# Attention with softmax rows copied from SBUF to SBUF, fp32r transposes of the copies, and rotary tables read back from memory tile by tile

## The chip, the core and the metric

The kernel runs on one core of a Trainium2 chip. The metric is the device time of one execution in microseconds; the median of three runs before the change is 1856.83 us (1856.04 to 1858.79). The core has TensorE (PE, with its weight loads as PEld), VectorE (DVE), ScalarE (ACT), GpSimd (POOL) and SyncE (SP), which here only issues transfers. Tiles live in SBUF, results of matmuls in PSUM, inputs and spilled tensors in the chip's memory.

## The reference

One layer of a diffusion backbone on 1024 latent tokens with 256 context tokens and model width 1024. A token-mixing part has a gated recurrence (4 heads) and grouped-query attention side by side; a channel-mixing part sends tokens to 16 experts. The attention is what the change touches:

```python
def qk_norm(aq, ak):
    return rms_norm(heads(aq, ATT_HEADS), q_norm_g), rms_norm(heads(ak, ATT_KV_HEADS), k_norm_g)
...
xqa = apply_axial_rope(xqa, cos, sin)
xka = apply_axial_rope(xka, cos, sin)
keys = jnp.concatenate([cka, xka], axis=1)
vals = jnp.concatenate([cva, heads(xav, ATT_KV_HEADS)], axis=1)
...
def one_block(qi):
    s = jnp.einsum("bqhgd,bkhd->bhgqk", qi, k, preferred_element_type=jnp.float32) * scale
    p = jax.nn.softmax(s, axis=-1)
    return jnp.einsum("bhgqk,bkhd->bqhgd", p.astype(v.dtype), v)
```

There are 8 query heads of width 64 in 2 groups, and 1280 keys.

## The kernel before

The precision is kept by splitting an fp32 number into a high part rounded to fp32r and the remainder (`split`, L92 and L93: a cast on ScalarE, a subtraction on VectorE), and by three matmuls per product (`mm3g`, L176 to L178).

The attention stage works through 16 tiles: 8 blocks of 128 queries times 2 groups of 4 heads (`seq`). The score row of a head has 1280 columns, in three segments of 512, 512 and 256 (`SEG`). For a tile, `softmax` does, for one head, six score matmuls (L786), three maxima on VectorE (L788), and three exponentials on ScalarE (L795), each into an SBUF tile `p` of its segment; every segment has a ring of 5, 6 or 7 such tiles. `turn` j (ten per tile) transposes 128 columns of all four heads on TensorE, fp32 against `ident` (L804), into one PSUM tile, which is split into `pT`. `values` j multiplies the two parts with the values (L814). `back` and `out_turn` turn the tile's output.

The tiles overlap. A tile's loop has 24 steps i: an even i below 20 emits `turn` i/2; the steps i = 1, 6, 11, 16 (`SI`) emit `softmax` of heads 0 to 3 of the **next** tile; odd i from 5 on emit `values`; each step also emits some matmuls of independent work (`fill.run`: projections and the branches). So turn 0 of a tile comes right after the loop of the tile before, and it reads segment 0 of all four heads. Below, (h, a) is the exponential of head h and segment a; turns 0 to 3 read a = 0, turns 4 to 7 a = 1, turns 8 and 9 a = 2.

TensorE's order is the order in which the code is written. The other engines' orders come from a scheduler that goes by priorities; `tc.high_priority(offset=HP)` puts an instruction ahead. SyncE's queue issues transfers in order, so that an entry that waits holds up those behind it. A transfer's completion is counted by one of eight semaphores (`DMAHW0` to `DMAHW7`) that are used in turn.

Queries: `q_vec` loads a block's queries (`aq`), normalises them and rotates them with the tables `cq` and `sq` (cosine and sine times the gains), which stay in SBUF as two tiles of 256 KB; `q_turn` transposes the result (fp32r, against `identr`). Block 0 and 1 are rotated on VectorE, the others on GpSimd.

Of the kernel before, what the change touches and what calls it, by code (L numbers as in the profile page):

```python
# [28 lines left out]
def view(t, off, dims):  # L29
    """The tile's partitions with free dimensions [stride, size] from element off on."""  # L30
    a = t if isinstance(t, bass.AP) else t[:]
    return bass.AP(tensor=a.tensor, offset=a.offset + off, ap=[list(a.ap[0])] + [list(d) for d in dims])
# [13 lines left out]
def _layer(tc, nc, top, A, out):  # L46
# [35 lines left out]
    def rsqrt(pool, ss, n, scale, name):  # L82
        """(ss * scale + eps) ** -0.5"""
# [6 lines left out]
    def split(hi, lo, src, eng=None):  # L90
        """hi: src rounded to the parts' width; lo: what is left (exact)."""
        nc.scalar.copy(hi, src)  # L92
        (eng or nc.vector).tensor_tensor(lo, src, hi.bitcast(F32), op=OP.subtract)  # L93
# [3 lines left out]
    class Fill:  # L97
        """Matmuls of independent work, emitted between the steps of a dependent chain: the time is the tensor engine's."""
# [27 lines left out]
        def flushed(self):  # L126
            """The PSUM bank is on its way out: no matmuls into it for some steps."""
            self.wait = self.pause
# [7 lines left out]
    class Stream:  # L136
        """The weight chunks of the first sub-layer in the order of their use; each is loaded one chunk ahead."""
# [18 lines left out]
    def wload(src, kt, ncols, rowlen, off, hl=None):  # L156
        """A chunk of a weight: kt row tiles of 128, ncols columns from off on; as hi and lo."""
# [14 lines left out]
    def mm3g(p, a, b, nk, first=True, last=True):  # L172
        """p += sum over k of a[k].T @ b[k]; a, b: pairs of functions of k giving the hi and lo parts."""
# [15 lines left out]
    # the tokens, halves of them apart: [half][hi, lo]  # L189
# [15 lines left out]
    def natural(hi, lo, emit, tiles):  # L205
        """Token rows on the partitions: emit(token tile, PSUM); ctx tiles are 0, 1, x tiles 2 to 9."""
# [10 lines left out]
    def transposed(hi, lo, m, emit, ctx, halves=(0, 1)):  # L217
        """Features on the partitions: emit(first token, number of tokens, PSUM)."""
# [23 lines left out]
    with ExitStack() as st:  # L242
# [11 lines left out]
        # token tile t is loaded, normalised and transposed beside these row tiles of w_mod (9: after them)  # L254
# [51 lines left out]
        # rows 0, 1: the products with the hi parts of silu(c), silu(c_ctx); rows 2, 3: with the lo parts  # L306
# [64 lines left out]
    def rope_swap(o, x, s, eng):  # L371
        """o = x with the halves of each axis exchanged, times s; [128, heads, 64] each."""
# [4 lines left out]
    def gain_rows(rows, n):  # L377
        """A head's gains on all partitions, and the same with the halves of each axis exchanged."""
# [8 lines left out]
    lbp = consts.tile([128, 2, 4], F32, name="lbp")  # L387
    lb1 = consts.tile([128, 2, 4], F32, name="lb1")
    with ExitStack() as st:
        pool = st.enter_context(mkpool("right", name="sa", bufs=2))  # L390
        pps = st.enter_context(mkpool(name="saps", bufs=1, space=PSUM))
        # lower bounds: a softmax over the two layers' logits, its first component
# [19 lines left out]
        # keys: norm, rotary embedding; values as they are  # L412
# [63 lines left out]
        # the other adaLN parameters, as one row  # L476
# [33 lines left out]
        # their sums over the partitions, piece j of 512 on row j  # L510
# [20 lines left out]
    with ExitStack() as st:  # L531
# [41 lines left out]
        for i in range(2):  # L573
            for c in range(4):
                # of the last chunk the first half of the tokens first: it makes room
# [53 lines left out]
        def states(h, K, Z, acc, tt):  # L629
# [17 lines left out]
            def advance(d, i0, cs, kt):  # L647
# [3 lines left out]
                for i, c in enumerate(cs):  # L651
# [4 lines left out]
                    else:  # L656
                        # the state before the next chunk
# [51 lines left out]
    sOA = spill.tile([4, 128, T], F32, name="sOA")  # L709
    sBA = spill.tile([8, 128, T], F32, name="sBA")  # L710
    BA, BR, direct = [], [], [None]
# [6 lines left out]
    with ExitStack() as st:  # L718
# [15 lines left out]
        cq = pool.tile([128, 8, 64], F32, name="cq")  # L734
        sq = pool.tile([128, 8, 64], F32, name="sq")
        for i, (n, a) in enumerate((("c_cos", cq), ("c_sin", sq))):
            nc.scalar.dma_start(a, A[n].rearrange("(t p) c -> p t c", p=128))
            (nc.gpsimd, nc.vector)[i].tensor_tensor(a, a, rows[:, i:i + 1].to_broadcast([128, 8, 64]), op=OP.mult)
        QT, SC = {}, {}
# [3 lines left out]
        def q_vec(t):  # L743
            eng = nc.vector if t in QV else nc.gpsimd
            x = pool.tile([128, 8, 64], F32, name="aq", tag="aq")
            nc.sync.dma_start(x, sAQ[t].rearrange("p (h d) -> p h d", h=8))
            a = pool.tile([128, 8, 64], F32, name="qa", tag="qa")
# [8 lines left out]
            eng.tensor_tensor(a, x, cq[:, t:t + 1].to_broadcast([128, 8, 64]), op=OP.mult)  # L756
            rope_swap(b, x, sq[:, t:t + 1].to_broadcast([128, 8, 64]), eng)
# [16 lines left out]
        SEG = ((0, 512, 5), (512, 512, 6), (1024, 256, 7))  # L774

        def softmax(t, g, h):
# [16 lines left out]
            for a, (c0, n, bufs) in enumerate(SEG):  # L793
                p = pool.tile([128, n], F32, name="p", tag="p%d" % a, bufs=bufs)
                nc.scalar.activation(p, ss[a], AF.Exp, bias=m[:, 7:8], scale=sc, accum_out=SU[t, g][:, a, h:h + 1])  # L795
                PT[t, g, h, a] = p
            hp.__exit__(None, None, None)

        HL, PV = {}, {}

        def turn(t, g, j):
            p = ps.tile([128, 4, 128], F32, name="ptp", tag="pt", bufs=NPT)
            for h in range(4):
                nc.tensor.transpose(p[:, h], PT[t, g, h, j // 4][:, (j % 4) * 128:(j % 4 + 1) * 128], ident)  # L804
# [45 lines left out]
        def branch_in():  # L850
            """The first half of the tokens makes room for the first branch's input."""
# [41 lines left out]
        for h in range(4):  # L893
            softmax(0, 0, h)
            fill.run(F1)
        for n, (t, g) in enumerate(seq):
# [3 lines left out]
            for i in range(20 + LAG - 1):  # L900
# [12 lines left out]
                if nxt and i in SI:  # L913
                    softmax(*nxt, SI.index(i))
# [27 lines left out]
    with ExitStack() as st:  # L942
# [4 lines left out]
        # the router on x1: its weights take the norm's gain and the scale; the shift gives a row  # L947
# [21 lines left out]
        # merged branches: [hi, lo][row tiles 0-3, 4-7][tokens 0-511, 512-1023]  # L969
# [525 lines left out]
```

## Time and profile before

| what | before |
|---|---|
| median of the runs | 1856.83 us |
| the profiled execution, its span | 1854.5 us |
| TensorE busy, share of the span | 1731.6 us, 93% |
| VectorE busy | 1331.0 us, 72% |
| ScalarE busy | 995.4 us, 54% |
| GpSimd busy | 273.7 us, 15% |
| DMA, mean over the span | 207 GB/s |

The profile is that of one execution on the chip; its span runs from the first to the last instruction, and the run's time is a little longer. A busy TensorE means that matmuls are in flight there; they overlap, so the distance from one's start to the next one's start is what a matmul costs. In the time of attention, about 600 to 1012 us, the DMA engines are nearly empty, while in the experts' part behind it they carry some 370 GB/s.

### The profile page before, as it was taken

What the parts mean: (1) busy time and instruction counts of PE and PEld (TensorE: products, weight loads), DVE (VectorE), ACT (ScalarE), POOL (GpSimd) and SP (SyncE); (2) the same over time, 40 slices, a digit from 0 to 9 for tenths busy, and PEclk for the clock granted to TensorE, in tenths of its full rate; (3) what the DMA queues carried; (4) which work ended last, traced back from release to release, by engine and by line L of the source; (5) the groups of instructions that cost most, each with busy time, mean ns of one, the idle gap of its engine ahead of it and who ended that gap; (6) DMA issues with size and microseconds to landing.
All of it is one profiled execution on the core that took longest, in us unless ns stands there. A gap on an engine that the chain in (4) does not pass through costs nothing. (4 is left out here: it accounts for less than half of the span.)

```text
span 1854.5 us, 26192 instructions
## 1 busy us (share of the span) xinstructions
PE 1731.6 (93%) x9820; PEld 1454.9 (78%) x9820; DVE 1331.0 (72%) x2000; ACT 995.4 (54%) x1632; POOL 273.7 (15%) x241
## 2 busy tenths in 40 slices
PE   5899999999999799999999999939999999999995
PEld 2798887899988678787787788828888888887774
DVE  6656323876766466777875664469999999998897
ACT  6422331322323367777876532227777777777665
POOL 3400001020000201111100332140011001001103
PEclk9899999999999999999999999959999999999998
DMA  8285445353332410101212776459999999999972
GB/s 326 93 309 208 171 140 198 106 174 103 103 117 81 130 43 29 46 29 58 89 51 87 261 262 238 159 187 358 378 379 371 379 379 374 376 379 379 370 261 101
DMA packets 206319, 383.87 MB, mean 207 GB/s; under 512 B 17488, under 2 KB 65568, under 8 KB 202864
## 3 DMA queue, kind: packets, MB, share of 16 engines
q1 hardware_dynamic: 194944, 360.92, 54.4%
q0 software_dynamic: 4832, 19.34, 3.8%
q10 hardware_dynamic: 6416, 1.94, 0.4%
q8 instruction: 77, 1.26, 0.3%
q14 instruction: 50, 0.41, 0.1%
HBM read 323.02 MB, written 59.13 MB: 206 GB/s over the span
## 5 line engine op out<-in xcount | busy, mean ns | idle before, releaser
L93 DVE TENSOR_TENSOR elo<-eraw,ehi 128x1024 fp32r<-128x1024 f32 x378 | 452.2, 1221 | 22.2 <-ACT ehi L92 14.4
L92 ACT CAST ehi<-eraw 128x1024 fp32r<-128x1024 f32 x384 | 383.6, 1047 | 86.6 <-PE pgu L178 48.5
L177 PE MATMUL pgu<-elo,xeT 128*128 128x512 f32 x512 | 203.7, 398 | 2.8 <-DVE elo L93 2.4
L176 PE MATMUL pgu<-ehi,xeT 128*128 128x512 f32 x512 | 204.9, 400 | 0.2 <-ACT xeT L92 0.2
L178 PE MATMUL pgu<-ehi,xeT 128*128 128x512 f32 x512 | 202.4, 395 | 0.0
L176 PE MATMUL pj<-hx,whi 128*128 128x512 f32 x448 | 185.4, 414 | 6.5 <-ACT stg L69 5.3
L178 PE MATMUL pj<-hx,wlo 128*128 128x512 f32 x448 | 175.8, 392 | 0.0
L177 PE MATMUL pj<-hx,whi 128*128 128x512 f32 x448 | 175.5, 392 | 0.0
L795 ACT ACTIVATE p<-s,m,qsc 128x512 f32<-128x512 f32 (+1 forms) x192 | 134.3, 713 | 17.7 <-DVE m L792 17.5
L788 DVE TENSOR_REDUCE m<-s 128x1 f32<-128x512 f32 (+1 forms) x192 | 104.3, 596 | 48.5 <-PE s L786 48.2
L176 PE MATMUL pj<-whi,hx 128*128 128x256 f32 x448 | 130.9, 292 | 3.6 <-DVE stg L541 1.9
L92 ACT CAST pT<-ptp 128x512 fp32r<-128x512 f32 x160 | 92.7, 595 | 71.9 <-PE ptp L804 71.8
L178 PE MATMUL pj<-whi,hx 128*128 128x256 f32 x448 | 128.1, 286 | 1.4 <-DVE hx L93 1.3
L93 DVE TENSOR_TENSOR pT<-ptp,pT 128x512 fp32r<-128x512 f32 x160 | 108.3, 685 | 29.2 <-ACT pT L92 28.5
L177 PE MATMUL pj<-wlo,hx 128*128 128x256 f32 x448 | 127.4, 284 | 0.0
L177 PEld LDWEIGHTS pgu<-elo,xeT 128*128 128x128 f32 x512 | 96.3, 188 | 29.0 <-DVE elo L93 8.0
L176 PEld LDWEIGHTS pgu<-ehi,xeT 128*128 128x128 f32 x512 | 96.9, 189 | 21.8 <-ACT xeT L92 0.5
L178 PEld LDWEIGHTS pgu<-ehi,xeT 128*128 128x128 f32 x512 | 96.2, 188 | 22.6 <-DVE xeT L93 0.4
L1385 POOL DMA_INDIRECT ACC<-ye,idx x15 | 34.7, 2316 | 474.9 <-DVE ye L1384 474.9
L176 PE MATMUL pye<-ehi,hdT 128*128 128x512 f32 x256 | 104.8, 409 | 0.0
L177 PE MATMUL pye<-elo,hdT 128*128 128x512 f32 x256 | 102.1, 399 | 1.2 <-DVE elo L93 1.2
L814 PE MATMUL pv<-pT,vs 128*128 128x512 f32 x320 | 102.2, 403 | 0.9 <-DVE pT L93 0.8
(365 smaller groups left out, 3919.7 us busy)
## 6 DMA issues: line engine op xcount, KB each, us to landing
eraw<-in_w_exp_gate SPq DMA_DIRECT2D x64, 1024.0 KB, 12.0
eraw<-in_w_exp_up SPq DMA_DIRECT2D x64, 1024.0 KB, 11.6
eraw<-in_w_exp_down SPq DMA_DIRECT2D x64, 1024.0 KB, 12.2
wm<-in_w_mod SPq DMA_DIRECT2D x24, 1024.0 KB, 6.9
raw<-in_w_in SPq DMA_DIRECT2D x21, 1024.0 KB, 6.1
sFK<-sg SPq DMA_DIRECT2D x32, 256.0 KB, 2.3
sGT<-stg SPq DMA_DIRECT2D x32, 256.0 KB, 2.1
sgm<-sGT SPq DMA_DIRECT2D x32, 256.0 KB, 3.8
```

Of the source, the lines that this page charges most:

```text
L92: nc.scalar.copy(hi, src)
L93: (eng or nc.vector).tensor_tensor(lo, src, hi.bitcast(F32), op=OP.subtract)
L176: nc.tensor.matmul(p, a[0](k), b[0](k), start=s, stop=False)
L177: nc.tensor.matmul(p, a[0](k), b[1](k), start=False, stop=False)
L178: nc.tensor.matmul(p, a[1](k), b[0](k), start=False, stop=e)
L788: nc.vector.tensor_reduce(m[:, a:a + 1], s, axis=AX.X, op=OP.max)
L795: nc.scalar.activation(p, ss[a], AF.Exp, bias=m[:, 7:8], scale=sc, accum_out=SU[t, g][:, a, h:h + 1])
L814: nc.tensor.matmul(PV[t, g].rearrange("p a b -> p (a b)"), VS[:, g, j], hl[i], start=(j == 0 and i == 0), stop=(j == 9 and i == 1))
L1385: nc.gpsimd.indirect_dma_start(out=ACC, out_offset=bass.IndirectOffsetOnAxis(ap=idx[:, :1], axis=0), in_=ye, in_offset=None, compute_op=OP ...
```

## The change

Four things are done.

1. After the exponential, each tile `p` is copied by a transfer from SBUF to SBUF, issued by SyncE with high priority, into a tile `pr` (`relay`). The rings of 5, 6 and 6 buffers are now those of the copies; each exponential has a single buffer per segment, which comes free when its copy has landed. Most copies follow their softmax; three are issued later in the loop (`LATE`): (2,1) at step 15, (2,2) and (3,2) at step 19.
2. `turn` transposes the copies as fp32r against `identr`, by reading the same bits under that type.
3. The rotary tables are multiplied by the gains in temporary tiles (which borrow buffers of `pT1`) and stored to memory (`sRT`).
4. `q_vec` loads the 64 KB slice of its block (`cs`) and rotates with it.

```diff
-        cq = pool.tile([128, 8, 64], F32, name="cq")
-        sq = pool.tile([128, 8, 64], F32, name="sq")
-        for i, (n, a) in enumerate((("c_cos", cq), ("c_sin", sq))):
+        for i, n in enumerate(("c_cos", "c_sin")):
+            a = pool.tile([128, 8, 64], F32, name="rt", tag="pT1", bufs=3)
             nc.scalar.dma_start(a, A[n].rearrange("(t p) c -> p t c", p=128))
             (nc.gpsimd, nc.vector)[i].tensor_tensor(a, a, rows[:, i:i + 1].to_broadcast([128, 8, 64]), op=OP.mult)
+            nc.sync.dma_start(sRT[:, :, i].rearrange("t p c -> p t c"), a)
...
             nc.sync.dma_start(x, sAQ[t].rearrange("p (h d) -> p h d", h=8))
+            cs = pool.tile([128, 2, 64], F32, name="cs", tag="cs", bufs=2)
+            nc.sync.dma_start(cs, sRT[t])
...
-            eng.tensor_tensor(a, x, cq[:, t:t + 1].to_broadcast([128, 8, 64]), op=OP.mult)
-            rope_swap(b, x, sq[:, t:t + 1].to_broadcast([128, 8, 64]), eng)
+            eng.tensor_tensor(a, x, cs[:, :1].to_broadcast([128, 8, 64]), op=OP.mult)
+            rope_swap(b, x, cs[:, 1:].to_broadcast([128, 8, 64]), eng)
...
-        SEG = ((0, 512, 5), (512, 512, 6), (1024, 256, 7))
+        SEG = ((0, 512, 5), (512, 512, 6), (1024, 256, 6))
+        NEW = {}
+
+        LATE = {(2, 1): 15, (2, 2): 19, (3, 2): 19}
...
-                p = pool.tile([128, n], F32, name="p", tag="p%d" % a, bufs=bufs)
+                p = pool.tile([128, n], F32, name="p", tag="p%d" % a)
...
-                PT[t, g, h, a] = p
+                NEW[h, a] = t, g, p
             hp.__exit__(None, None, None)
+
+        def relay(h, a):
+
+            t, g, p = NEW.pop((h, a))
+            n = SEG[a][1]
+            r = pool.tile([128, n], F32, name="pr", tag="pr%d" % a, bufs=SEG[a][2])
+            with tc.high_priority(offset=HP):
+                nc.sync.dma_start(r, p)
+            PT[t, g, h, a] = r
...
-                nc.tensor.transpose(p[:, h], PT[t, g, h, j // 4][:, (j % 4) * 128:(j % 4 + 1) * 128], ident)
+                nc.tensor.transpose(p[:, h].bitcast(F32R), PT[t, g, h, j // 4][:, (j % 4) * 128:(j % 4 + 1) * 128].bitcast(F32R), identr)
...
                 if nxt and i in SI:
-                    softmax(*nxt, SI.index(i))
+                    h = SI.index(i)
+                    softmax(*nxt, h)
+                    for a in range(3):
+                        if (h, a) not in LATE:
+                            relay(h, a)
+                if nxt:
+                    for k, at in LATE.items():
+                        if at == i:
+                            relay(*k)
```

TensorE at the border of the seventh tile, before: the last values of the tile that ends, then turn 0, which reads segment 0 of four heads (`p_7217` is head 3's), then the scores of the following tile's head 0. In brackets stands what a row waits for.

```order
L814 MATMUL pv_7078<-pT_7233,vs_5357 128x512 [waits Activation_49]
L814 MATMUL pv_7078<-pT_7234,vs_5357 128x512 [waits DVE_49]
L804 MATMUL ptp_7272<-ident_71,p_7032 128x128 [waits PE_49]
L804 MATMUL ptp_7272<-ident_71,p_7104 128x128
L804 MATMUL ptp_7272<-ident_71,p_7158 128x128
L804 MATMUL ptp_7272<-ident_71,p_7217 128x128 [waits Activation_49]
L786 MATMUL s_7283<-kT_5355,qT_6939 128x512 x2
L786 MATMUL s_7287<-kT_5355,qT_6939 128x512 [waits Activation_49]
```

The same place after the change (`pr_7394` is the copy of head 3's):

```order
L830 MATMUL pv_7239<-pT_7408,vs_5358 128x512 [waits Activation_49]
L830 MATMUL pv_7239<-pT_7409,vs_5358 128x512 [waits DVE_49]
L820 MATMUL ptp_7453<-identr_78,pr_7193 128x128 [waits DMAHW7_49,PE_49]
L820 MATMUL ptp_7453<-identr_78,pr_7271 128x128 [waits DMAHW2_49]
L820 MATMUL ptp_7453<-identr_78,pr_7331 128x128 [waits DMAHW6_49]
L820 MATMUL ptp_7453<-identr_78,pr_7394 128x128 [waits DMAHW1_49]
L793 MATMUL s_7464<-kT_5356,qT_7084 128x512 [waits Activation_49]
L793 MATMUL s_7464<-kT_5356,qT_7084 128x512
```

TensorE's order is the same; the wait of the fourth transpose is for a transfer and no longer for ScalarE, and the other three have one too.

SyncE's queue before, around that border: stores of staged tiles, a query load and a weight chunk.

```order
L847 DMA sOA_5348<-stg_6604 128x2x128 [waits DMAHW0_49,Activation_49]
L70 DMA sGT_2588<-stg_6652 128x512 [waits DMAHW1_49,Activation_49]
L746 DMA aq_7251<-sAQ_2589 128x512 [waits DMAHW5_49,DMAHW2_49,Pool_49]
L70 DMA sGT_2588<-stg_6854 128x512 [waits DMAHW3_49,Activation_49]
L164 DMA raw_7761<-in_w_branch_a 128x4x512 [waits DMAHW4_49,DVE_49]
L847 DMA sOA_5348<-stg_6871 128x2x128 [waits Activation_49]
```

And after, the copies of heads 1, 2 and 3 of the seventh tile, with what lies between and behind them:

```order
L812 DMA pr_7271<-p_7265 128x512 [waits DMAHW2_49,PE_49,Activation_49]
L812 DMA pr_7273<-p_7267 128x512 [waits DMAHW3_49,Activation_49]
L812 DMA pr_7275<-p_7269 128x256 [waits DMAHW4_49,Activation_49]
L863 DMA sOA_5348<-stg_7308 128x2x128 [waits DMAHW5_49,Activation_49]
L812 DMA pr_7331<-p_7325 128x512 [waits DMAHW6_49,PE_49,Activation_49]
L812 DMA pr_7358<-p_7327 128x512 [waits DMAHW7_49,PE_49,Activation_49]
L812 DMA pr_7412<-p_7329 128x256 [waits DMAHW0_49,PE_49,Activation_49]
L812 DMA pr_7394<-p_7388 128x512 [waits DMAHW1_49,Activation_49]
L812 DMA pr_7396<-p_7390 128x512 [waits DMAHW2_49,Activation_49]
L812 DMA pr_7414<-p_7392 128x256 [waits DMAHW3_49,PE_49,Activation_49]
L70 DMA sGT_2588<-stg_7489 128x512 [waits DMAHW4_49,Activation_49]
L748 DMA aq_8017<-sAQ_2589 128x512 [waits DMAHW5_49,Pool_49]
```

Twelve copies a tile stand among the same stores and loads; the two late ones of head 2 (`pr_7358`, `pr_7412`) wait for TensorE and stand ahead of head 3's first.

VectorE at the start of attention, before: the sine table times the gains, the rotation of block 0, the remainder of its split (`qs`), then block 1.

```order
L738 TENSOR_TENSOR sq_5386<-sq_5386,rows_5379 128x512 [waits DMAHW5_49,DMAHW3_49,DMAHW7_49,DMAHW1_49,DMAHW0_49]
L375 TENSOR_TENSOR qb_5404<-aq_5391,sq_5386 128x16x16 [waits DVE_49]
L375 TENSOR_TENSOR qb_5404<-aq_5391,sq_5386 128x16x16
L758 TENSOR_TENSOR qa_5393<-qa_5393,qb_5404 128x512 [waits DVE_49]
L93 TENSOR_TENSOR qs_5409<-qa_5393,qs_5409 128x8x64 [waits Activation_49]
L748 TENSOR_TENSOR qa_5680<-aq_5678 128x512 [waits DMAHW1_49,DVE_49]
```

And after:

```order
L739 TENSOR_TENSOR rt_5390<-rt_5390,rows_5380 128x512 [waits DMAHW5_49,DMAHW3_49,DMAHW7_49,DMAHW1_49,DMAHW0_49]
L760 TENSOR_TENSOR qa_5398<-aq_5394,cs_5396 128x512 [waits DMAHW4_49,DVE_49]
L375 TENSOR_TENSOR qb_5409<-aq_5394,cs_5396 128x16x16 x2
L762 TENSOR_TENSOR qa_5398<-qa_5398,qb_5409 128x512 [waits DVE_49]
L93 TENSOR_TENSOR wlo_5550<-raw_5548,whi_5549 128x2048 [waits PE_49,Activation_49]
L93 TENSOR_TENSOR qs_5414<-qa_5398,qs_5414 128x8x64 [waits Activation_49]
```

The rotation now waits for the slice `cs` (`DMAHW4`), which in turn is loaded after both stores of `sRT`, and the remainder of a weight chunk (`wlo`) has come to stand ahead of `qs`.

## Rows read from the trace of the kernel before

**Rows 1.** Attention by engine: window, us, busy, PEclk, DMA share, GB/s.

```profile
657.00:1012.00 355.00, 347.88 (x1942) 282.90 (x1941) 259.95 (x585) 261.62 (x620) 37.44 (x38) 1.00 0.16 52
```

**Rows 2.** Groups in 657 to 1012: busy us, mean ns, idle before.

```profile
L804 PE MATMUL ptp<-ident,p 128*128 128x128 f32 x640 | 96.2, 273 | 3.3 <-DVE pT L93 2.8
```

**Rows 3.** TensorE's waits in 657 to 1012: total us, times, longest.

```profile
PE ptp L804 <- DVE pT L93: 2.8, 3, 1.7
...
PE pv L814 <- ACT pT L92: 0.2, 1, 0.2
```

**Rows 4.** Timeline of TensorE at a border: start, us, instruction, count.

```profile
765.17 1.42 PE L786 MATMUL s<-kT,qT 128*128 128x512 f32 x6
...
767.58 0.60 PE L804 MATMUL ptp<-ident,p 128*128 128x128 f32 x4
767.94 0.47 PE L176 MATMUL pj<-hx,whi 128*128 128x512 f32 x1
768.25 0.39 PE L177 MATMUL pj<-hx,whi 128*128 128x512 f32 x1
...
770.80 0.60 PE L804 MATMUL ptp<-ident,p 128*128 128x128 f32 x4
```

**Rows 5.** Timeline of TensorE where keys are transposed as fp32r.

```profile
269.89 0.46 PE L458 MATMUL ptk<-identr,kd 128*128 128x128 f32 x4
270.18 0.46 PE L176 MATMUL pj<-hx,whi 128*128 128x512 f32 x1
270.48 0.40 PE L177 MATMUL pj<-hx,whi 128*128 128x512 f32 x1
```

**Rows 6.** Timeline of ScalarE at the border of rows 4: (3,0).

```profile
768.70 0.79 ACT L795 ACTIVATE p<-s,m,qsc 128x512 f32<-128x512 f32 x1
769.38 0.20 ACT L795 ACTIVATION_READ_ACCUMULATOR p<-s,m,qsc 128x1 f32 x1
```

**Rows 7.** Timeline of ScalarE: (3,0) at the loosest and the tightest border.

```profile
834.26 0.82 ACT L795 ACTIVATE p<-s,m,qsc 128x512 f32<-128x512 f32 x1
...
993.89 0.78 ACT L795 ACTIVATE p<-s,m,qsc 128x512 f32<-128x512 f32 x1
```

**Rows 8.** Timeline of TensorE: turn 0 at these two borders.

```profile
838.08 0.60 PE L804 MATMUL ptp<-ident,p 128*128 128x128 f32 x4
...
995.30 0.60 PE L804 MATMUL ptp<-ident,p 128*128 128x128 f32 x4
```

**Rows 9.** Transfers in 657 to 1012: count, KB each, median us to landing.

```profile
sGT<-stg SPq DMA_DIRECT2D x14, 256.0 KB, 2.0
...
sOA<-stg SPq DMA_DIRECT2D x10, 128.0 KB, 1.8
aq<-sAQ SPq DMA_DIRECT2D x5, 256.0 KB, 2.7
raw<-in_w_in SPq DMA_DIRECT2D x1, 1024.0 KB, 5.2
...
stg<-sOA SPq DMA_DIRECT2D x4, 64.0 KB, 2.0
...
hd<-sMod SPq DMA_DIRECT2D x1, 8.0 KB, 1.5
```

**Rows 10.** Timeline of VectorE at the start of attention.

```profile
623.11 0.69 DVE L738 TENSOR_TENSOR sq<-sq,rows 128x512 f32<-128x512 f32 x1
...
624.63 0.69 DVE L758 TENSOR_TENSOR qa<-qa,qb 128x512 f32<-128x512 f32 x1
626.01 0.69 DVE L93 TENSOR_TENSOR qs<-qa,qs 128x512 fp32r<-128x512 f32 x1 [0.69 <-ACT qs L92]
...
636.67 2.28 DVE L93 TENSOR_TENSOR wlo<-raw,whi 128x2048 fp32r<-128x2048 f32 x1
```

**Rows 11.** Timeline of TensorE there: queries turned, first scores, a later wait.

```profile
628.10 0.79 PE L769 MATMUL ptq<-identr,qs 128*128 128x128 f32 x8
633.62 2.50 PE L786 MATMUL s<-kT,qT 128*128 128x512 f32 x6 [4.73 <-DVE qT L770]
...
645.51 0.50 PE L176 MATMUL pj<-hx,whi 128*128 128x512 f32 x1 [1.28 <-ACT stg L69]
```

More of the change, by code (lines that the diff above doesn't have):

```diff
@@ L710, in _layer @@
     sBA = spill.tile([8, 128, T], F32, name="sBA")
+    sRT = spill.tile([8, 128, 2, 64], F32, name="sRT")
     BA, BR, direct = [], [], [None]
@@ L913, in _layer @@
                 if nxt and i in SI:
-                    softmax(*nxt, SI.index(i))
+                    h = SI.index(i)
+                    softmax(*nxt, h)
+                    for a in range(3):
+                        if (h, a) not in LATE:
+                            relay(h, a)
+                if nxt:
+                    for k, at in LATE.items():
+                        if at == i:
+                            relay(*k)
                 fill.run(FB if BR else FA)
```

## The prediction

> **What bounds the kernel now.** I read the views in this order: the busy times of the attention stage, its costliest groups on TensorE, TensorE's waits there, the timelines of TensorE and ScalarE around the border between two tiles, the landing times of transfers, and the start of the stage. In the 355 us from 657 to 1012, which hold fifteen borders between the sixteen tiles, TensorE is busy for 347.88 us at full granted clock, VectorE and ScalarE for about 260 each, and the DMA engines carry 52 GB/s at a share of 0.16 [rows 1]. Its waits there are short: five groups that sum to 6.6 us, of 2.8, 1.7, 1.1, 0.8 and 0.2 [rows 3]. So the stage costs what its matmuls cost. A saving on TensorE counts in full, and so does any new wait of TensorE. That makes the border the place to look at: TensorE's order is fixed by hand, and its order there is score matmuls of head 3 of the next tile, fillers and value matmuls, then turn 0 of that next tile, which reads the exponentials of all four heads.
>
> **The transposes.** The 640 transposes of softmax rows are fp32 [rows 2]. Four of them start at 767.58 and the next matmul at 767.94, and that one's successor at 768.25: 0.36 + 0.31 = 0.67 us [rows 4]. A group of four fp32r transposes in the same position, also followed by L176 and L177, starts at 269.89, 270.18 and 270.48: 0.29 + 0.30 = 0.59 us [rows 5]. That is 0.08 us less for a group of four, and 160 groups give **-12.8 us**. The times are rounded to a hundredth, so I keep -10.5 to -15. All of it lies on the path, apart from what the borders take back.
>
> **The copies.** Each of the 192 exponential tiles gets a transfer from SBUF to SBUF, and what follows reads the copy. For most of them there is time: from border to border a tile takes 22.5 us ((995.30 - 838.08) / 7 [rows 8]), so its 24 steps take 0.94 each, and turns 4 and 8, which are the first to read the second and third segments, come 8 and 16 steps after turn 0. Turn 0 is different. At a typical border the exponential (3,0) runs from 768.70 to 769.49 and its accumulator is read out by 769.58 [rows 6]; turn 0 starts at 770.80 [rows 4], which is 1.31 us after the exponential ends. The same difference read at all fifteen borders is, in order, 1.31, 1.88, 1.40, 2.00, 1.31, 1.33, 1.79, 2.99, 1.31, 1.32, 1.02, 1.05, 1.88, 1.36, 0.63 us. The longest is from 834.26 + 0.82 on ScalarE to 838.08, the shortest from 993.89 + 0.78 to 995.30 [rows 7, 8]. In the changed order only the last of turn 0's four transposes reads head 3, and each of the four waits for its own transfer.
>
> No transfer from SBUF to SBUF stands in this trace. The nearest rows: stores of 256 KB land 2.0 us after issue, stores of 128 KB 1.8, loads of 256 KB 2.7, a load of 8 KB 1.5 [rows 9]. The copy is 256 KB and its source is SBUF like that of the 256 KB store, so I take 2.0 and keep 1.5 and 2.7 as ends. From the end of the exponential the copy needs 0.1 (accumulator), 0.2 (two handovers, an estimate) and the landing L. Three transposes that go ahead give 0.2 back, and the one turn between these points that has become shorter takes 0.08. So TensorE waits L + 0.18 less the slack, where that is positive. Summed over the fifteen slacks: 10.9 us for L = 2.0, 4.8 for 1.5, 8.2 for 1.8, 20.7 for 2.7. **+10.9 us.** Behind the waiting transpose stand, on TensorE, the score matmuls of the following tile's head 0 and all else, since that order is fixed; ScalarE and VectorE wait for these in turn.
>
> The Trainium skill, page "DMA: Bandwidth & Descriptors", section "Anatomy of one DMA — SWDGE (gpsimd) path", gives 2.0 us plus bytes over 436e3 per microsecond, 2.6 us for 256 KB (an estimate from that page), though for transfers issued another way. The trace's 256 KB stores land in 2.0, so the measurement speaks against the second part of the sum; by the page the wait would be about 19 us.
>
> **What the borders pay back.** A TensorE that pauses at turn 0 lets VectorE and ScalarE catch up, and the 6.6 us of waits for them [rows 3] shrink. I take about half, **-3 us** (0 to -6.6).
>
> **SyncE's queue.** All copies are issued by SyncE in order, together with the stores of staged tiles, the query loads and the weight chunks, and each waits for the transfer eight before it. Late copies are placed where their buffers have come free: (2,1) after turn 7, (2,2) after turn 9, both ahead of (3,0), and both turns end before that exponential does, so I see no standing block. The DMA engines at a share of 0.16 [rows 1] have room for the copies: 128 of 256 KB and 64 of 128 KB are 41.9 MB, in 355 us 118 GB/s. But a weight chunk of 1 MB, landing in 5.2 us [rows 9], would hold up a copy at a border by up to 3.2 us if it falls there. Five such chunks in the stage, and a chance of about 5.2 of 22.5 us for each, with stores in front of a copy now and then: **+2 us** (0 to +6). More waits on one instruction and ScalarE's exponentials, which now wait until the copy from the single buffer has landed (for (3,2) about 2 to 3 us after turn 9, just long enough): **+0.5** (0 to +2.5).
>
> **The rotary tables.** Before, the sine table's product ends at 623.80, tile 0's queries are rotated by 625.32 and split by 626.70, and TensorE turns them at 628.10, when it gets to it [rows 10, 11]. Now the product is stored (256 KB, 2.0) and a 64 KB slice comes back (2.0) [rows 9]: about 628.4 with handovers. Three products, 0.7 to 0.8 each, end at 630.6. In the changed order the 2.28 us remainder of a weight chunk (`wlo`, at 636.67 before [rows 10]) stands ahead of the queries' remainder, which ends near 633.6. TensorE turns then instead of at 628.10, and the first scores start near 635.6 instead of 633.62: +2.0. Of the 1.28 us at 645.51, a wait for a ScalarE copy [rows 11] that the changed order puts earlier, some 0.5 goes. **+1.5 us** (-1 to +5). The slices of later tiles come beside a 256 KB query load that takes longer, so they cost nothing; without that cover each would cost under 2 us, seven times.
>
> **Sum.** -12.8 + 10.9 - 3.0 + 2.0 + 0.5 + 1.5 = -0.9 us. The profiled execution spans 1854.5 us and the median of the runs is 1856.8, so 2.3 us lie around the span and stay: **1855.9 us**.
>
> **The rivals.** What a measurement of this kernel can tell from no change is about 0.2%, 3.7 us.
> First, the forecast: the border gives back nearly what the transposes win. Chance 0.41 (about 0.35 within 0.2%, 0.03 on each side).
> Second, the copy lands sooner than a store, in 1.5 to 1.8 us; for it speaks that neither end is in memory, against it that the only row below 1.8 carries 8 KB. Then the border costs 4.8 to 8.2 and the time is 1849.8 to 1853.2, say 1851. Chance 0.32, nearly all faster.
> Third, slower: the copies land like the 256 KB loads, 2.7 us, at every border. One mechanism: the last transpose of turn 0 waits 1.57 us at a typical border. It decides from L of about 2.3, where the border's cost passes 15 us and the sum is above +3.5. The sum becomes -12.8 + 20.7 + 1 = +8.9 and the time 1865.7. For it: 192 copies more than triple what the DMA engines carry; against it: at 52 GB/s even stores of that size land in 2.0. Chance 0.18. The Trainium skill's formula from the page named above would land here, at 2.6 us.
> Fourth, SyncE's order: a copy (3,0) stands at every border behind a store that waits for ScalarE, a microsecond each, +15 in all: 1870.9. Chance 0.05.
> Fifth, the change does not do what it says: fp32r transposes on copied data step like fp32 ones, 0.67 us for four. The 12.8 is lost: 1868.7. The key transposes at 0.59 speak against it. Chance 0.04.
>
> **How the numbers follow.** Faster by over 0.2%: 0.29 + 0.03 = 0.32. Slower by over 0.2%: 0.15 + 0.05 + 0.04 + 0.03 = 0.27. The rest, 0.41, is within. The range of the likeliest case alone is 1852 to 1860; the range over the cases goes from the second's lower end, with a little more from the transposes, to just past the third: 1848 to 1867.
>
> **What would show it.** Copies near 2.0 us in the list of transfers. In the timeline of TensorE a gap of 0.5 to 1.2 us before the last transpose of turn 0, put down to the transfer `pr<-p`, at twelve or more borders, and waits for transfers near 11 us in all. Groups of four transposes at 0.59 with their follower. The first scores about 2 us later than before, measured from the sine product. Wrong would be: no such waits (the second), waits near 20 us (the third), gaps on SyncE behind stores (the fourth), fours that still take 0.67 (the fifth). A longer stage with no waits on TensorE at the borders would overturn the whole reading.

## The result

The changed kernel takes 1872.65 us (median of 4 runs, 1871.05 to 1876.09), the kernel before in the same comparison 1856.43; the ratio is 1.0085, with a 95% interval of 1.0070 to 1.0101. That is 16.2 us slower, 13.0 to 18.8 by the interval. The prediction was 1855.9 us, no change, with a range of 1848 to 1867; the result lies above the range, and where the sum had -0.9 us the kernel became slower.

The profiled execution spans 1872.3 us, 17.8 more than before. Since TensorE runs its matmuls in the same order in both kernels, the timelines can be laid on each other matmul by matmul. Up to the 25th matmul ahead of the first turn of queries, a point shortly ahead of attention, the changed kernel is 4.1 us behind, from there to the last softmax transpose it loses 13.4 (387.7 us before, 401.1 after), and behind that 0.3. The 4.1 us lie in code that the change leaves alone. They come mostly with stretches at the lower granted clock, one early in the program and one from 617 us on, and in the other kernels of this study, which have the same code there, the same point comes between 0.8 us earlier and 9.0 us later than in the kernel before. So all comparisons of traces below are made on the attention stretch, from that 25th matmul to the last transpose.

TensorE in attention by engine as in [rows 1] (window, us, busy of PE, PEld, DVE, ACT, POOL, clock, DMA share, GB/s), from the first turn of softmax rows to the last, before and after:

```profile
657.50:1009.10 351.60, 344.48 (x1925) 280.15 (x1924) 258.91 (x583) 260.94 (x617) 37.44 (x38) 1.00 0.16 52
661.80:1026.60 364.80, 340.71 (x1925) 269.48 (x1924) 260.73 (x584) 262.57 (x619) 37.52 (x38) 1.00 0.46 160
```

TensorE is busy for 3.8 us less and the stretch is 13.2 longer all the same: it stands idle for 24 us, where it was 7. The waits of TensorE there, which answer to [rows 3] (waiting tile and line, what ended the wait: total us, times, longest):

```profile
PE ptp L820 <- DMA pr<-p: 12.4, 15, 1.9
PE s L793 <- ACT p L802: 5.3, 7, 1.2
PE ptp L820 <- DVE pT L93: 3.1, 3, 1.9
PE pj L176 <- ACT stg L69: 1.1, 4, 0.4
PE pv L830 <- DVE pT L93: 0.8, 2, 0.6
PE ptp L820 <- DVE m L799: 0.7, 3, 0.2
PE pv L830 <- ACT pT L92: 0.3, 1, 0.3
```

The first row is new, the second has grown from 1.7, the rest is near what it was. A border looks like this in the timeline of TensorE (start, us, instruction, count, idle time before and its releaser):

```profile
683.32 0.63 PE L830 MATMUL pv<-pT,vs 128*128 128x512 f32 x2
683.79 0.37 PE L820 MATMUL ptp<-identr,pr 128*128 128x128 f32 x3
684.86 0.28 PE L820 MATMUL ptp<-identr,pr 128*128 128x128 f32 x1 [0.70 <-DMA pr<-p]
684.97 0.46 PE L176 MATMUL pj<-hx,whi 128*128 128x512 f32 x1
```

and in that of ScalarE, exponential (3,0) of the same tile:

```profile
681.60 0.79 ACT L802 ACTIVATE p<-s,m,qsc 128x512 f32<-128x512 f32 x1
```

The exponential ends at 682.39, turn 0 starts at 683.79 (a slack of 1.40, against 1.31 at this border before), three transposes go ahead, and the fourth starts at 684.86, 2.47 us after the exponential. Landing times of the transfers in the stage (KB each, median us from issue to landing), as in [rows 9]:

```profile
pr<-p SPq DMA_DIRECT2D x122, 256.0 KB, 2.3
pr<-p SPq DMA_DIRECT2D x62, 128.0 KB, 2.1
sGT<-stg SPq DMA_DIRECT2D x15, 256.0 KB, 2.1
...
raw<-in_w_branch_a SPq DMA_DIRECT2D x2, 1024.0 KB, 5.3
```

Laid on each other, the 13.4 us come out as follows, each figure a sum of differences between starts of neighbouring matmuls: the transposes with the matmul behind each group -9.4; the longest step inside turn 0 at the fifteen borders +14.5; score matmuls that come late +5.6; the first turn of queries with the first scores +0.8; all else +1.9. Such sums depend by some tenths on where a step is booked.

### The profile page after: what moved, and what is told of

The parts are those of the page before. It is cut to its first block, busy times and chain, and to the rows that moved or that the text cites. A ratio compares the mean times of both kernels' runs of the same rounds, so it can differ in the third digit from the quotient of the medians.

```text
span 1872.3 us, 26764 instructions
## 1 busy us (share of the span) xinstructions
PE 1731.7 (92%) x9819; PEld 1447.0 (77%) x9820; DVE 1332.5 (71%) x2000; ACT 997.2 (53%) x1632; POOL 274.2 (15%) x241
## 5 line engine op out<-in xcount | busy, mean ns | idle before, releaser
L69 ACT COPY stg<-pj 128x512 f32<-128x512 f32 (+1 forms) x92 | 46.3, 504 | 110.6 <-PE pj L178 88.2
## 6 DMA issues: line engine op xcount, KB each, us to landing
eraw<-in_w_exp_down SPq DMA_DIRECT2D x64, 1024.0 KB, 12.2
```

Of the source, the lines that this page charges most:

```text
L69: (eng or nc.scalar.copy)(x[:, :n], p)
```

## The experiments

The table gives the ratio to the kernel before, measured beside it, with its 95% interval, and the length of the attention stretch in the one profiled execution. These lengths hold zero to four short stretches at the lower clock behind the first turn of softmax rows; where it matters below, that is said.

| kernel | ratio | attention, us |
|---|---|---|
| before | 1 | 387.7 |
| after | 1.0085 (1.0070 to 1.0101) | 401.1 |
| copies, fp32 transposes | 1.0113 (1.0090 to 1.0135) | 407.0 |
| rounded exponentials, no copies | 0.9976 (0.9964 to 0.9987) | 379.9 |
| tables only | 1.0008 (0.9993 to 1.0022) | 387.8 |
| last exponential read directly | 0.9999 (0.9978 to 1.0020) | 385.3 |
| chunks from GpSimd | 1.0096 (1.0068 to 1.0124) | 407.2 |
| filler moved to the border | 1.0074 (1.0047 to 1.0101) | 406.1 |
| last read directly, chunks from GpSimd | 0.9993 (0.9980 to 1.0006) | 388.2 |
| rounded, one value matmul | 0.9807 (0.9782 to 0.9831) | 348.3 |
| segments 1 and 2 copied, two buffers | 0.9987 (0.9975 to 0.9999) | 383.9 |
| segments 1 and 2 copied, one buffer | 0.9996 (0.9984 to 1.0008) | 384.3 |

**Copies, fp32 transposes.** Against the changed kernel:

```diff
-nc.tensor.transpose(p[:, h].bitcast(F32R), PT[t, g, h, j // 4][:, (j % 4) * 128:(j % 4 + 1) * 128].bitcast(F32R), identr)
+nc.tensor.transpose(p[:, h], PT[t, g, h, j // 4][:, (j % 4) * 128:(j % 4 + 1) * 128], ident)
```

> The change with one part undone: the copies and the rotary tables stay as changed, the 640 transposes read the copies as fp32 against ident, as before. Theory (the loss is 14.5 us of waits of turn 0 for the last copy, 4 to 5 us at the start of attention and 5 to 6 us of score matmuls that wait for exponentials, less what the shorter transposes give): the transposes cost 9 to 11 us more than in the changed kernel, so 1881 to 1884 us, and the waits for copies at the borders go from 14.5 to about 13. Rival (fp32r transposes gave nothing, the whole +16 is the net of smaller waits): 1872 to 1874.

Measured: 1877.04 us (1872.2 to 1880.28) against 1857.5, so 19.5 us over the kernel before, where the changed one is 16.2 over it: between theory and rival, and the two intervals overlap. The attention stretch is 5.9 us longer than the changed kernel's; the transposes alone cost 10.9 us more, and the longest steps at the borders 1.2 less:

```profile
PE ptp L820 <- DMA pr<-p: 10.4, 11, 1.9
PE s L793 <- ACT p L802: 4.4, 7, 1.2
```

The price of the copies, with the tables, is therefore 19 us in the trace and 19.5 in the medians. Of the 10.9 us that fp32r gives 5.9 are left in the trace; much of the rest is waits, 4.1 us more of them in the changed kernel: slower transposes leave shorter waits behind them.

**Rounded exponentials, no copies.** Against the kernel before. ScalarE itself rounds the exponentials to fp32r here and nothing is copied, where the changed kernel copies them as they are; what is left out is the remainder of the softmax weights below fp32r:

```diff
-p = pool.tile([128, n], F32, name="p", tag="p%d" % a, bufs=bufs)
+p = pool.tile([128, n], F32R, name="p", tag="p%d" % a, bufs=bufs)
...
-nc.tensor.transpose(p[:, h], PT[t, g, h, j // 4][:, (j % 4) * 128:(j % 4 + 1) * 128], ident)
+nc.tensor.transpose(p[:, h].bitcast(F32R), PT[t, g, h, j // 4][:, (j % 4) * 128:(j % 4 + 1) * 128], identr)
```

> The kernel before with fp32r transposes and no copies: ScalarE writes the exponentials already rounded to fp32r, so the remainder of a softmax weight is left out of what is computed; the tables stay on chip. It shows the transposes' gain alone. Theory: 9 to 11 us off, 1845 to 1848 us, borders without waits for transfers, groups of four transposes at 0.06 us each and 0.37 us with the delay of the next matmul against 0.44. Rival (shorter transposes only uncover waits for ScalarE and VectorE that were hidden): under 4 us off, 1853 or more, and TensorE's waits in the stage grow from 6.6 us by the difference.

Measured: a ratio of 0.9976, 4.5 us off (2.4 to 6.7), just above what the rival allowed and half of the theory's. In the trace the transposes give 10.4 us with the matmuls behind them, near the changed kernel's 9.4, and the stretch is 7.8 us shorter. But 2.4 of the 7.8 lie at the first scores: after a stretch at the lower clock, with a mean of 0.57 from 619 to 623 us, TensorE came there late and waited 2.30 us, where it was 4.73 [rows 11]. From the first turn of softmax rows to the last the gain is 4.4, like that of the medians. Of what is missing a part is new waits: in that stretch they are 10.3 us, before 6.6 [rows 3]; another 1.3 us goes with a stretch at the lower clock near 910 us. The wait at the first scores, and the rows that have grown:

```profile
636.18 2.23 PE L786 MATMUL s<-kT,qT 128*128 128x512 f32 x6 [2.30 <-DVE qT L770]
...
PE pj L176 <- ACT stg L69: 2.2, 6, 0.9
PE ptp L804 <- DVE m L792: 2.1, 5, 1.2
```

So the rival was right in part: shorter work on TensorE uncovers waits for ScalarE and VectorE.

**Tables only.** The kernel before with the diff's lines on `sRT`, `rt` and `cs`, and none of the others.

> The kernel before with the rotary tables alone stored and read back, no copies, fp32 transposes. Theory (the round trip of the tables delays the first scores, and the delay of 4.3 us at the first turn in the changed kernel is mostly this): 1858.5 to 1861 us, the first scores 3 to 5 us later than at 633.62. Rival (most of that delay was other: a later load of values, TensorE at its lower clock after a longer wait): 1856 to 1857.5.

Measured: 1.0008, not told apart from no change. The first scores come 13.6 us behind the 25th matmul ahead of the query turn, where it was 12.2, and TensorE's wait has moved ahead of that turn (compare [rows 11]):

```profile
632.39 1.25 PE L772 MATMUL ptq<-identr,qs 128*128 128x128 f32 x8 [4.90 <-DVE qs L93]
634.27 2.50 PE L789 MATMUL s<-kT,qT 128*128 128x512 f32 x6 [0.62 <-DVE qT L773]
```

The stretch is 387.8 us, as before: 1.4 us lost there, and 1.2 gained at the wait at 645.51 in [rows 11]. By the first scores, which come 0.65 us later than at 633.62 and not 3 to 5, the theory fell, though the interval of the time alone would allow it; most of the late start of the changed kernel's profile was there ahead of attention, with the lower clock.

**Last exponential read directly.** Against the changed kernel, with two buffers for segment 0's exponentials and four for its copies:

```diff
+            if (h, a) == (3, 0):
+                PT[t, g, h, a] = p
+                return
...
+                if (h, j // 4) == (3, 0):
+                    nc.tensor.transpose(p[:, h], PT[t, g, h, j // 4][:, (j % 4) * 128:(j % 4 + 1) * 128], ident)
+                else:
```

> The changed kernel, but the first segment of head 3 is not copied: turns 0 to 3 read that one exponential directly as fp32 (2 buffers for it, 4 for the copies of this segment), 176 of the 192 copies stay. Theory (the loss at a border is the landing of the last copy): the 14.5 us of waits for transfers at turn 0 fall below 2, 64 fp32 transposes beside fp32r ones cost 3 to 6 us, so 1860 to 1865 us. Rival (the traffic of the copies slows the stage as a whole): 15 of 16 of the loss stays, 1870 to 1874.

Measured: 0.9999 (0.9978 to 1.0020), the loss gone within 4 us, with 176 of 192 copies still made. The attention stretch is 15.8 us shorter than the changed kernel's. No wait for a transfer is left, the waits for exponentials stay:

```profile
PE s L793 <- ACT p L802: 4.4, 5, 1.5
PE ptp L826 <- DVE pT L93: 4.1, 3, 1.9
```

This decides between the border and the traffic: the loss sits in the sixteen copies that the next transposes need at once. The time came out below the 1860 to 1865 us that were expected: the 64 fp32 transposes among fp32r ones don't show their 3 to 6 us.

**Chunks from GpSimd.** Four of the five weight chunks of 1 MB are issued on GpSimd's queue in this stage; the last, at 994.75, is still issued by SyncE:

```diff
-        nc.sync.dma_start(f(raw), dram(src, off, [[rowlen, 128], [128 * rowlen, kt], [1, ncols]]))
+        LQ[0].dma_start(f(raw), dram(src, off, [[rowlen, 128], [128 * rowlen, kt], [1, ncols]]))
...
+        LQ[0] = nc.gpsimd
```

> The changed kernel, but the weight chunks of 1 MB that are loaded during attention are issued by GpSimd on its own queue and no longer by SyncE. Theory (score matmuls wait because an exponential waits for its single buffer, whose copy stands behind a chunk in SyncE's queue): TensorE's waits for exponentials, 5.3 us in the changed kernel, fall to about 2, those for copies at the borders stay at 12 to 15, the time falls by about 3 us against the changed kernel. Rival (the chunk takes the same 16 engines whoever issues it, so its copies are as late): waits for exponentials stay at 5 or more, and the time stays within 1 us of the changed kernel's.

Measured: 1.0096, not better than the changed kernel, and the waits for exponentials became longer:

```profile
PE ptp L821 <- DMA pr<-p: 12.0, 14, 1.9
PE s L794 <- ACT p L803: 6.4, 6, 2.9
```

The longest, 2.9 us, ends at 698.15, behind the chunk issued at 689.36: ScalarE sat idle for 5.3 us until the copy that held the single buffer, issued at 690.17, had landed after 6.96 us. In the changed kernel the same place, after the chunk at 690.29, cost 1.2 us. So a chunk does delay copies, as the theory has it, but another queue is no remedy; the rival holds on the waits, and its time, within 1 us of the changed kernel, can't be told at this noise. The stretch of 407.2 us in the table is not the price of the edit: three more stretches at the lower clock than in the changed kernel, near 925, 1003 and 1017 us, cost 1.5 us each against the same matmuls there.

**Filler moved to the border.** Against the changed kernel:

```diff
-                fill.run(FB if BR else FA)
+                fill.run((FB if BR else FA) * (0.82 if i < 20 else 1.9))
```

> The changed kernel with independent matmuls moved towards the border: in a tile's steps 20 to 23 the filler's allowance is 1.9 times what it was, in the steps before 0.82 times, the sum is the same. About 0.9 us more work then lies between the last scores and turn 0. Theory (the border costs the landing of the last copy less the slack there): the 14.5 us of waits for copies fall to 2 to 5, some 2 to 4 us come back as waits for ScalarE and VectorE in the thinner steps, 1862 to 1866 us. Rival (any slack is used up by later copies, or the stage is bound elsewhere): 1870 or more.

Measured: 1.0074, within the interval of the changed kernel's ratio. The waits for copies fall as expected, and come back elsewhere:

```profile
PE s L793 <- ACT p L802: 5.2, 8, 1.2
PE pj L176 <- ACT stg L69: 4.6, 8, 0.7
PE ptp L820 <- DVE pT L93: 4.0, 3, 1.8
PE ptp L820 <- DMA pr<-p: 3.6, 3, 2.1
PE pv L830 <- DVE pT L93: 3.1, 6, 0.6
PE ptp L820 <- DVE m L799: 1.9, 8, 0.2
```

From 12.4 to 3.6 for copies, but 19.2 us for ScalarE and VectorE where it was 11.3, so that the sum, 22.8 us, is nearly the changed kernel's 23.7. The stretch in this profile is even 5 us longer than the changed kernel's, which is about what the lower clock takes: it has a mean of 0.83 in four windows of 10 us between the first turn and the last, where the changed kernel has one such; one of the four:

```profile
780.00:790.00 10.00, 9.18 (x46) 7.21 (x46) 6.96 (x16) 5.16 (x12) 0.00 (x0) 0.83 0.25 92
```

The theory was right on the border and wrong on the time, and the rival's 1870 or more holds: the fillers that were moved had been hiding other waits.

**Last read directly, chunks from GpSimd.** Both edits at once.

> Two edits at once: the first segment of head 3 is read directly as fp32, and the weight chunks of the attention stage are issued by GpSimd. Theory: the gains add up, 15 us from the first and 2 to 3 from the second, so 2 to 3 us under the kernel before, 1853 to 1856. Rival (they overlap or the second gives nothing): within 1 us of the kernel before.

Measured: 0.9993 (0.9980 to 1.0006), not told apart from the first edit alone; the waits for exponentials are 6.2 us in all, the longest 2.9, as with the chunks alone. The second edit gives nothing that can be told here, as the rival had it.

**Rounded, one value matmul.** The rounded kernel from above, in which the remainder is zero, so that its subtraction and its matmul go:

```diff
...
-            split(hl[0], hl[1], p.rearrange("p a b -> p (a b)"))
+            nc.scalar.copy(hl[0], p.rearrange("p a b -> p (a b)"))
...
-            for i in range(2):
-                nc.tensor.matmul(PV[t, g].rearrange("p a b -> p (a b)"), VS[:, g, j], hl[i],
-                                 start=(j == 0 and i == 0), stop=(j == 9 and i == 1))
+            nc.tensor.matmul(PV[t, g].rearrange("p a b -> p (a b)"), VS[:, g, j], hl[0], start=(j == 0), stop=(j == 9))
```

> The kernel with exponentials written as fp32r, no copies, fp32r transposes, and as the remainder of such a weight is zero, its subtraction on VectorE and the second value matmul are left out (160 of each). What is left out of the computation is the remainder of the softmax weights. Theory (TensorE bounds the stage): 160 matmuls at 0.23 us, 37 us, and the transposes' 4 us come off, less new waits: 1815 to 1825. Rival (with less work on TensorE the score chain through VectorE and ScalarE bounds the tile): 1830 to 1845.

Measured: 1823.62 us, ratio 0.9807 (0.9782 to 0.9831), 35.5 us under the kernel before and inside the theory's range. The stretch is 31.6 us shorter than that of the rounded kernel with two matmuls:

```profile
662.90:977.80 314.90, 300.17 (x1768) 239.44 (x1766) 165.47 (x423) 258.95 (x617) 39.10 (x38) 0.99 0.17 58
```

VectorE's busy time falls to 165 us from the 260 of [rows 1], TensorE still bounds the stage. This is the fastest kernel of the study, at a price in precision that neither of the two kernels pays.

**Segments 1 and 2 copied.** No copy for segment 0: turns 0 to 3 read fp32, turns 4 to 9 fp32r copies. Twins with two buffers and with one for segment 1's exponentials:

```diff
+            if a == 0:
+                PT[t, g, h, a] = p
+                return
...
-                p = pool.tile([128, n], F32, name="p", tag="p%d" % a)
+                p = pool.tile([128, n], F32, name="p", tag="p%d" % a, bufs=(5, 2, 1)[a])
```

> The changed kernel, but segment 0 of no head is copied: turns 0 to 3 read the exponentials directly as fp32 (5 buffers), turns 4 to 9 read copies as fp32r; segment 1's exponentials have two buffers, segment 2's one. Theory (what a copy costs is the time to the turn that reads it, and these copies have 8 steps or more): no waits for copies at turn 0, six tenths of the transposes' 9 to 10 us come off, waits for exponentials near the 1.7 us of the kernel before; 1 to 5 us under the kernel before. Rival (the traffic and SyncE's longer queue cost by themselves): at or above the kernel before, with waits that grew by 5 us or more.

> As the run with segments 1 and 2 copied, with a single buffer for segment 1's exponentials too. Theory (the single buffer makes an exponential wait for the copy of the head before, and score matmuls for it): waits of score matmuls for exponentials 1 to 3 us above the twin with two buffers, and the time above it by as much. Rival (these waits come from ScalarE's order and not from the buffers): the same waits and time in both, within 0.5 us of waits.

Measured: 0.9987 (0.9975 to 0.9999) and 0.9996 (0.9984 to 1.0008). With two buffers, where the theory holds, the transposes give 6.7 us (11.1 less 4.4 on the matmuls behind them), the stretch is 3.8 us shorter than before, and the waits are near [rows 3]:

```profile
PE ptp L824 <- DVE pT L93: 2.8, 3, 1.7
PE s L793 <- ACT p L802: 2.4, 5, 0.8
PE pj L176 <- ACT stg L69: 1.0, 4, 0.3
```

128 copies with 8 steps or more of time cost nearly nothing, which speaks against the traffic a second time. With one buffer, score matmuls wait 0.7 us longer in all (3.1 against 2.4) and the stretch is 0.3 longer: the single buffer of segment 1 alone explains little. The theory of the second twin, 1 to 3 us, is not borne out, its rival (0.5) is nearer.

## Why the prediction was wrong

**What bounds the stage** was read rightly: TensorE, whose every new wait counts, with the border as the place. The step that failed most is the credit for waits: the sum booked -3 us for waits of TensorE that would shrink and +2.5 for queue and buffers, and these waits grew. Transposes and border were mis-sized besides, and every error but one pointed the same way.

**The transposes**, -12.8, gave -9.4 in the changed kernel and -10.4 where nothing is copied. The group in the changed kernel steps like the fp32r keys of [rows 5], as forecast:

```profile
695.06 0.45 PE L820 MATMUL ptp<-identr,pr 128*128 128x128 f32 x4
695.35 0.47 PE L176 MATMUL pj<-hx,whi 128*128 128x512 f32 x1
695.66 0.39 PE L177 MATMUL pj<-hx,whi 128*128 128x512 f32 x1
```

That is 0.29 + 0.31 = 0.60 against 0.67 in [rows 4], 0.07 and not 0.08, and over all groups 0.06. Mis-sized by 3.4 us, outside the bound of 10.5: a difference of rounded times was multiplied by 160.

**The border**, +10.9, was +14.5. At eleven of the fifteen borders the forecast held, 8.7 us in sum and 8.9 measured, but in part by luck: two of its terms were off in opposite directions. An undisturbed copy of 256 KB landed in 2.27 us and not in 2.0; on the other side the copy was issued 0.11 us after the exponential's end, and at the two borders where the landing can be read the transpose came 0.04 to 0.05 behind it, in place of 0.3 for accumulator and handovers. The missing 3.4 us stand at the other four borders, 5.6 where 2.2 were forecast. From the issue of copy (3,0) to the fourth transpose it took 2.30 to 2.39 us at ten borders, and 2.71, 2.81, 3.20 and 4.26 at these four; at the loosest there is no wait. So what the step lacked is not a longer landing everywhere but late copies at a few borders. At the three longest a packet of another queue moved meanwhile (last section); ahead of the one of 2.71 a store of 256 KB had been issued 0.77 us before the copy, the "stores in front of a copy" that the prediction put into its +2.

None of the rivals is this. The third, with a chance of 0.18, comes nearest by its sign, but it wanted a late landing at every border and decides from a border's cost of 15 us, which was not reached; it ended 7 us too low although its border cost 20.7. Even with 14.5 for the border the prediction's own sum gives +2.7 us, 1859.5, inside its range.

**What the borders pay back**, -3, is the step that had the wrong sign. Waits for ScalarE and VectorE did not shrink from 6.6 us; they are 11.3 in the changed kernel. Copies without shorter transposes raise them to 9.2 (copies, fp32 transposes), shorter transposes without copies to 10.3 (rounded exponentials). The waits for `pT` and for staged tiles, 2.8 and 1.1 before, are 3.1 and 1.1 after, so the pause at turn 0 took nothing off them. Why not is argued and was not tried: the places where TensorE waited in [rows 3] come later in the tile and may be set by chains that start behind the pause.

**SyncE's queue and the buffers**, +2 and +0.5: the first was looked for at the border, where no chunk fell. The chunks were felt elsewhere, in the exponentials, which wait until the copy of the head before has left the single buffer; the 0.5 had that place and was too small. The score matmuls' longer steps sum to +5.6; the waits for exponentials alone, 5.3 against 1.7, are 3.6 of it. Of the 5.6, 1.9 us stand behind the chunk of 690.29. The timeline of SyncE there (issue times):

```profile
690.29 0.39 SPq L164 DMA_DIRECT2D raw<-in_w_in  x1
691.38 6.79 SPq L812 DMA_DIRECT2D pr<-p  x4
```

and ScalarE's:

```profile
696.81 0.78 ACT L802 ACTIVATE p<-s,m,qsc 128x512 f32<-128x512 f32 x1 [0.67 <-DMA pr<-p]
```

Another step, longer by 1.5 us, of which 0.5 comes back right behind it, stands at 1000.83, behind the chunk issued at 993.39, and there ScalarE does not wait for a copy but comes late in its own order. In all of attention ScalarE waits for a copy three times, 1.5 us together, so most of the 5.6 is no direct wait for a buffer. How the rest divides between late copies and ScalarE's order was not settled; the twins show that the one buffer of segment 1 is not much of it, and with two buffers for segment 0 (last exponential read directly) 4.4 us of such waits remain.

**The rotary tables**, +1.5, cost nothing that can be measured in the time. In the run with the tables alone the first scores lost 1.4 us and not 2.0, and the wait at 645.51 gave 1.2 back and not 0.5.

**The sum.** On the attention stretch, -0.9 was forecast and 13.4 came: of the 14.3 between them 3.4 lie in the transposes and 3.6 in the border, 3.0 were booked as paid back and were not, by 3.1 the score matmuls' 5.6 exceed the 2.5 set for queue and buffers, 1.9 is spread over all else, and 0.7 less was lost at the first query turn. The measured 16.2 is 2.8 more than the stretch accounts for; that lies inside the interval, and the code outside the stretch is the same, so nothing more is claimed for it.

The Trainium skill, page "DMA: Bandwidth & Descriptors", section "Anatomy of one DMA — SWDGE (gpsimd) path", gives 2.6 us for 256 KB by its formula (an estimate from that page); the copies, issued in another way, landed in 2.27, between it and the prediction's 2.0. The same section says that the wait for a write to be confirmed is longest when memory is the target. This case's trace does not agree, as far as whole landing times can tell: undisturbed stores of 256 KB to memory landed in 1.99 to 2.01 us and copies of 256 KB into SBUF in 2.25 to 2.29, both issued by SyncE.

## What to carry to other kernels

A copy cost nothing that could be measured where its reader comes late, and its landing less the slack where the reader comes next. So count for each copy the time from its source to its first reader, and leave out those that don't have it: 128 of the 192 copies were worth making here, by a narrow margin, and the sixteen that the next transposes need cost more than all the transposes gained. Where a transfer stands on the path many times, price the late ones apart from the typical one: four of fifteen borders held nearly all that the border cost beyond the forecast. And don't book a credit for waits that a new pause or a shorter step might absorb: in every kernel here but the one with the tables alone, the waits for other engines stood above those of before, at 7.3 to 19.2 us against 6.6. Before two traces are compared, count the stretches at the lower clock in both.

## What was not expected of the hardware

A copy of 256 KB from SBUF to SBUF took longer than a store of the same size to memory, 2.27 us against 2.0. At the border of 751 to 756 us it was 4.26 us from the copy's issue to the transpose, and a packet of another queue, which carries instructions, moved in that time (from 751.7 to 756.1):

```profile
q1 hardware_dynamic: 441, 0.66, 41.5%
q8 instruction: 1, 0.02, 2.0%
```

(queue: packets, MB, share of 16 engines). A share of 2.0% of 16 engines in 4.4 us is 1.4 us on one of them. By the times of the packets it runs from 753.01 to 754.40, and behind it the transfers' queue, busy until then, moves single packets that start at 754.40, 754.61, 754.82 and 755.03. Such a packet stands at four borders. At the three longest (2.81, 3.20, 4.26 us) it starts 0.08, 0.20 and 1.23 us after the copy's issue; at the fourth it starts 1.98 us after it, and the copy took 2.35. All four fit a packet that holds up those of the copy that are still to move on its engine; no run without it was made.

After the longest wait at a border the granted clock dropped: TensorE had stood still for 1.92 us up to 756.04, and the window from 755 to 758 has a mean granted clock of 0.70, that is, a part of it at the lower of the two levels, 1.2 GHz:

```profile
755.00:758.00 3.00, 1.96 (x6) 1.58 (x7) 0.63 (x1) 0.59 (x1) 0.00 (x0) 0.70 0.15 53
```

It does not drop behind every such wait: TensorE stood still for 1.93 us up to 925.14 in the same trace, and from 925 to 935 the clock has a mean of 1.00; in the kernel with chunks from GpSimd it dropped after that same wait. So a wait near 2 us can cost more than its own length, by the 1.5 us that were read off there, and a variant that trades one wait for several, as the moved filler does, can lose by the clock what it wins.
